# Experts in pairs with one branch between them, and one arm for the further tokens of both

## The chip, the cores and the metric

The kernel runs on one core of a Trainium2 chip. TensorE (PE) multiplies, VectorE (DVE) and ScalarE (ACT) work on what it leaves in the accumulators, GpSimd (POOL) does little here, and SyncE (SP) issues the DMA transfers. The metric is device time of one launch in microseconds (us), lower is better.

## The reference

Two layers over 256 tokens of width 1024. Each layer is an attention (differential in the first, stick-breaking in the second) and a layer norm, then a mixture of 32 experts and a layer norm. The change touches the experts alone:

```python
    g_prob = jax.nn.softmax((xt @ w_group + b_group).astype(f32), axis=-1)
    g_gate, g_idx = lax.top_k(g_prob, 1)
    ...
    e_gate, e_idx = lax.top_k(e_prob, MOE_TOP_K)
    ...
    def step(acc, ew):
        w1e, w3e, w2e, ge = ew
        h = jax.nn.silu(xt @ w1e) * (xt @ w3e)
        return acc + ge[:, None] * (h @ w2e).astype(f32), None
    y, _ = lax.scan(step, jnp.zeros((t, d), f32), (w1, w3, w2, gates.T))
```

Only the tokens with a gate above zero need an expert's work. How many these are is known on the chip alone, after the router. With the inputs of these runs the counts, which the reference's own router gives, are, for experts 0 to 31:

```
layer 0: 25 10 6 1 4 4 3 21 | 98 11 114 36 13 19 4 23 | 10 4 1 12 1 2 5 3 | 15 6 7 0 19 17 14 4
layer 1: 8 1 3 9 2 1 12 4 | 11 37 16 16 3 30 18 43 | 27 29 19 14 43 28 73 9 | 10 5 4 2 10 3 15 7
```

So in layer 0 experts 8 and 10 have over 96 tokens and expert 11 has 36; in layer 1 expert 22 has 73, and 9, 15 and 20 have 37 to 43. All the others fit into 32.

## The kernel before

**The stream.** An expert's weights are six tiles of 1 MB (w1, w3, w1, w3, w2, w2). Sixteen ring slots and four other places (T12, `wl`, `wh`, `x`) hold 20 tiles, a little over three experts. SP issues all transfers, in one fixed order. `refill` (line 148) hands each place that comes free to the next tile in the queue, so tile n stands in the place that tile n − 20 had, and SP waits at its issue until PE has read that older tile for the last time. Eight DMA semaphores are used in turn, so at most eight transfers are in flight.

**An expert.** The tokens that an expert serves are picked by a matmul with a matrix of ones and zeros (`oh`): `gather` (from line 840) does it for the 64 first tokens of each of four experts at once, after every fourth expert, and its marks `oh` are made by VectorE at line 843. Then PE multiplies into w1 and w3 ("up", line 923), VectorE and ScalarE copy the result, PE turns it (936), ScalarE and VectorE make silu times linear, PE multiplies into w2 ("down", 950), and the result with its gates is spread back over the tokens (`combine`, 872), one expert later for the short forms.

**The two forms and their branch.** There is a form for 32 tokens (64 matmuls of 128x256 up) and one for 64 (32 of 128x512). From expert 1 on each expert has a branch of its own (line 1093, on PE, ACT and DVE): over 32 tokens the 64-token form is run, and inside it, between up and the rest, `overflow` (line 1050) has a branch for over 64 tokens (1051), within it one for over 128 (1053) and one for over 192 (1055). An overflow gathers its 64 tokens (`gather_over`, 967) and runs the 64-token form on them, using the weights in their slots. `foresee` tells PE's sequencer ahead of time which way a branch will go (a hint); the branches at 1053 and 1055 have no hint. Expert 0 runs the 32-token form with no branch; its further tokens are done at expert 1 (`rest_of_first`), by a branch in which SP and its transfers take part.

A branch with all its transfers on SP makes SP wait at its end until all transfers in flight have landed:

```python
            n = count(0, ET.SP)
            with tc.If(n > 32):
                more(0, 32, w1, w3, w2, 32)
```

## Time and profile before

| | |
|---|---|
| median of 3 runs | 1286.6 us (1285.23 to 1286.78) |
| the profiled execution | 1279.04 us, its span 1277.3 us |
| granted clock of TensorE, mean of the span | 0.911 |
| moved by DMA | 443.12 MB |
| experts of layer 0, of layer 1 | about 152 to 642, 790 to 1262 us of the span |

The rows further below come from the profiled execution, with times in us from the start of its span. The experts of both layers are a steady stream of weights at around 0.41 MB a microsecond while the DMA engines are busy. The attention stages lie before 152, and between 642 and 790.

### The profile page before, as it was taken

What the parts mean: (1) busy time and instruction counts of PE and PEld (TensorE: products, weight loads), DVE (VectorE), ACT (ScalarE), POOL (GpSimd) and SP (SyncE); (2) the same over time, 40 slices, a digit from 0 to 9 for tenths busy, and PEclk for the clock granted to TensorE, in tenths of its full rate; (3) what the DMA queues carried; (4) which work ended last, traced back from release to release, by engine and by line L of the source; (5) the groups of instructions that cost most, each with busy time, mean ns of one, the idle gap of its engine ahead of it and who ended that gap; (6) DMA issues with size and microseconds to landing.
All of it is one profiled execution on the core that took longest, in us unless ns stands there. A gap on an engine that the chain in (4) does not pass through costs nothing. (4 is left out here: it accounts for less than half of the span.)

```text
span 1277.3 us, 21392 instructions
## 1 busy us (share of the span) xinstructions
PE 1028.1 (80%) x8502; PEld 631.0 (49%) x8502; DVE 401.9 (31%) x972; ACT 261.1 (20%) x625; POOL 143.5 (11%) x127
## 2 busy tenths in 40 slices
PE   8997887679877776877999998877867768866875
PEld 7886644434343443534468975444443434433542
DVE  5777612111121111213177766212121111111213
ACT  2344312111111111111112443111111111111111
POOL 4343000000000000004033320000000000000501
PEclk8998989898899878879999999979997998889898
DMA  7994689999499999999997337899999999999991
GB/s 251 353 374 158 201 323 414 413 372 389 168 365 411 415 406 411 410 409 416 404 383 282 127 123 279 303 412 413 402 416 398 408 408 410 415 396 399 386 411 44
DMA packets 102379, 443.12 MB, mean 347 GB/s; under 512 B 19016, under 2 KB 20080, under 8 KB 60288
## 3 DMA queue, kind: packets, MB, share of 16 engines
q1 hardware_dynamic: 102144, 439.98, 87.7%
q8 instruction: 148, 2.42, 0.8%
q14 instruction: 87, 0.71, 0.2%
HBM read 438.88 MB, written 1.06 MB: 344 GB/s over the span
## 5 line engine op out<-in xcount | busy, mean ns | idle before, releaser
L923 PE MATMUL bA<-w,T 128*32 128x256 f32 (+1 forms) x3128 | 285.4, 442 | 93.5 <-issue 51.9
L923 PEld LDWEIGHTS bA<-w,T 128*32 128x32 f32 (+1 forms) x3128 | 138.4, 123 | 212.1 <-issue 165.8
L950 PE MATMUL bY<-w,T 128*32 128x512 f32 (+1 forms) x864 | 138.7, 634 | 3.3 <-DVE T L944 1.9
L931 DVE COPY T<-bA 128x128 f32<-128x128 f32 (+1 forms) x64 | 19.6, 306 | 338.4 <-PE bA L923 292.8
L954 DVE SCALAR_TENSOR_TENSOR T<-bY,gv,T 128x512 fp32r<-128x512 f32 x64 | 48.1, 751 | 239.7 <-ACT T L953 239.7
L293 POOL TENSOR_TENSOR wl<-w,wh 128x512 fp32r<-128x512 f32 x66 | 86.8, 1316 | 187.8 <-DVE wh L292 82.5
L932 ACT COPY T<-bA 128x128 f32<-128x128 f32 (+1 forms) x64 | 17.7, 277 | 427.0 <-DVE T L931 422.2
L1006 POOL PARTITION_BROADCAST wh<-wh x8 | 5.6, 799 | 834.0 <-DMA wh<-in_ln_mix_b_dram 834.0
L856 PE MATMUL bA<-oh,xh 128*128 128x256 f32 x224 | 65.7, 323 | 31.5 <-DVE oh L843 30.5
L953 ACT ACTIVATE T<-bY,gv 128x512 fp32r<-128x512 f32 x64 | 44.0, 687 | 215.0 <-PE bY L950 215.0
L872 PE MATMUL bS<-T,gT 64*128 64x512 f32 x512 | 84.9, 449 | 0.7 <-DVE T L954 0.5
L856 PEld LDWEIGHTS bA<-oh,xh 128*128 128x128 f32 x224 | 48.9, 218 | 46.3 <-issue 42.5
L950 PEld LDWEIGHTS bY<-w,T 128*32 128x32 f32 (+1 forms) x864 | 31.2, 119 | 68.1 <-issue 48.4
L856 PE MATMUL bA<-oh,xl 128*128 128x256 f32 x224 | 63.5, 309 | 0.0
L293 DVE TENSOR_TENSOR wl<-w,wh 128x512 fp32r<-128x512 f32 x62 | 52.8, 851 | 19.2 <-ACT wh L292 17.3
L872 PEld LDWEIGHTS bS<-T,gT 64*128 64x128 f32 x512 | 47.3, 200 | 20.7 <-issue 12.5
L944 DVE TENSOR_TENSOR T<-T,bA 128x128 f32<-128x128 f32 (+1 forms) x64 | 19.3, 302 | 94.5 <-ACT T L943 94.5
L856 PEld LDWEIGHTS bA<-oh,xl 128*128 128x128 f32 x224 | 49.1, 219 | 0.0
L885 PE MATMUL bA<-ident,gg 128*128 128x128 f32 x128 | 30.3, 320 | 23.2 <-DVE T L931 14.7
L347 PE MATMUL bA<-xh,wh 128*128 128x256 f32 x160 | 47.1, 294 | 1.1 <-ACT xh L292 0.7
L349 PE MATMUL bA<-xl,wh 128*128 128x256 f32 x160 | 46.2, 289 | 0.9 <-DVE xl L293 0.9
L923 PE MATMUL bA<-T,T 128*32 128x256 f32 (+1 forms) x240 | 35.6, 444 | 13.4 <-issue 8.3
(301 smaller groups left out, 1690.5 us busy)
## 6 DMA issues: line engine op xcount, KB each, us to landing
w<-in_moe_w_dram SPq DMA_DIRECT2D x311, 1024.0 KB, 16.2
T<-in_moe_w_dram SPq DMA_DIRECT2D x48, 512.0 KB, 7.8
wl<-in_moe_w_dram SPq DMA_DIRECT2D x64, 256.0 KB, 12.0
wh<-in_moe_w_dram SPq DMA_DIRECT2D x64, 256.0 KB, 8.0
x<-in_moe_w_dram SPq DMA_DIRECT2D x16, 1024.0 KB, 9.5
w<-in_da_wk_dram SPq DMA_DIRECT2D x4, 1024.0 KB, 15.8
w<-in_da_wv_dram SPq DMA_DIRECT2D x4, 1024.0 KB
w<-in_da_wo_dram SPq DMA_DIRECT2D x4, 1024.0 KB, 15.2
```

What stands on the lines that cost most here:

```text
L293: lo.tensor_tensor(dl, src, dh.bitcast(F32), op=OP.subtract)
L347: nc.tensor.matmul(o, wh[:, cs], xh[:, k, :], start=k == 0 and cb % 2 == 0, stop=False, skip_group_check=True)
L349: nc.tensor.matmul(o, wh[:, cs], xl[:, k, :], start=False, stop=False, skip_group_check=True)
L856: nc.tensor.matmul(ps[:, kk * 256:kk * 256 + 256], part[:, t, c], oh[:, t].rearrange("p e c -> p (e c)"), start=n == 0, stop=n == 3)
L872: nc.tensor.matmul(acc[t][h], gT[r, t * P:(t + 1) * P], y[r, :], start=False, stop=last and y is yl, skip_group_check=True, tile_position= ...
L885: nc.tensor.transpose(ps[:, t * P:(t + 1) * P], gg[:, t], ident)
L923: nc.tensor.matmul(ps[j * C:(j + 1) * C, 0:W], xs(k), w(k % 4, j2 * W, (j2 + 1) * W), start=k == 0, stop=k == KC - 1, skip_group_check=Tru ...
L931: nc.vector.tensor_copy(ud[:, :, 0], us[:, :, :, 0])
L944: nc.vector.tensor_tensor(hT, s, pv[:, :, 64:P], op=OP.mult)
L950: nc.tensor.matmul(ps[j * C:(j + 1) * C, :], hT[:, c, q * C:(q + 1) * C], w2[m // 2](m % 2, h * 512, (h + 1) * 512), start=c == 0, stop=c ...
L953: nc.scalar.activation(yh, ps, AF.Copy, scale=gs)
L954: nc.vector.scalar_tensor_tensor(yl, ps, gs, yh.bitcast(F32), op0=OP.mult, op1=OP.subtract)
```

## The change

Experts go in pairs (even, odd). The even expert always runs the 32-token form with no branch, the odd one's branch asks whether either of the two has over 32 tokens. Where not, the odd one's 32-token form follows. Where so, the arm first does the even expert's further tokens (`rest(e - 1, ...)`), then the odd one's, and then the odd one's 32-token form. `rest` has three ways: up to 64 further tokens wanted (33 to 64 in all) a second 32-token run on the tokens that are already gathered; up to 96 one gather and one 64-token run; more (to 160) the arm v, with two gathers and two 64-token runs in turns. What is over 160 (or over 32 in expert 0) is done at expert 15, by a branch `z` over all experts in which SP takes part. `expert` is cut into `up`, `take_up`, `turn_up`, `glu`, `down` and `store`, so that `in_turns` can interleave two runs. Slots of the even expert are refilled behind the odd one, with the odd one's. The marks of a gather are made before the odd expert, and the gather runs behind it as before.

```diff
-        def gather(g):
+        def group_marks(g):
             oh = ph.tile([P, NT, GRP, CAP], F32R, name="oh")
             for t in range(NT):
                 nc.vector.tensor_tensor(oh[:, t], io[:, None, 0:CAP].to_broadcast([P, GRP, CAP]),
                                         pos[:, t, g * GRP:(g + 1) * GRP, None].to_broadcast([P, GRP, CAP]),
                                         op=OP.is_equal)
+            return oh
+
+        def gather(oh):
...
+        def in_turns(e, C, ggm, U, xm, w1, w3, w2, out):
+            pt = bankA()
+            turn_up(U[:, 0:HID], pt, HID)
+            pb = bankY()
+            up(e, CAP, lambda k: xm[:, k, :], w1, w3, pb, "m")
+            hT = glu(pt, U[:, 0:HID], HID)
+            outm = outputs(e, "m")
+            take_up(U[:, HID:], pb, HID)
+            gates(e, ggm, outm[0], outm[1], bankY)
+            pt = bankY()
+            turn_up(U[:, HID:], pt, HID)
+            ya = bankY()
+            down(CAP, hT, w2, ya)
+            hT = glu(pt, U[:, HID:], HID)
+            store(out, ya)
+            yb = bankY()
+            down(CAP, hT, w2, yb)
+            store(outm, yb)
+            return outm
...
+        def rest(e, n, xg, c0, w1, w3, w2, out, ahead=None):
+            with tc.If(n < CAP + 1):
+                foresee("u", e, n, CAP)
+                expert(e, 32, 32, lambda k: xg[k // 4][:, k % 4, c0 + 32:c0 + 64], w1, w3, w2, "", out)
+                combine(*out)
+            with tc.If(n > CAP, label=f"u{layer}_{e}"):
+                with tc.If(n < 32 + CAP + 1):
+                    foresee("v", e, n, 32 + CAP)
+                    more(e, 32, w1, w3, w2)
+                with tc.If(n > 32 + CAP, label=f"v{layer}_{e}"):
+                    if ahead is not None:
+                        ahead()
+                    oh = over_marks(e, io[:, 32:32 + CAP], CAP, "m")
+                    gg = marks(e, 32, CAP, "")
+                    both = blk(3, 2)
+                    xa = gather_over(oh, CAP, both[:, 0])
+                    over_marks(e, io[:, 32 + CAP:32 + 2 * CAP], CAP, "m", oh)
+                    ggm = marks(e, 32 + CAP, CAP, "m")
+                    pa = bankA()
+                    up(e, CAP, lambda k: xa[:, k, :], w1, w3, pa, "")
+                    U = blk(8, 1)[:, 0]
+                    take_up(U[:, 0:HID], pa, HID)
+                    xm = gather_over(oh, CAP, both[:, 1])
+                    gates(e, gg, out[0], out[1], bankA)
+                    outm = in_turns(e, CAP, ggm, U, xm, w1, w3, w2, out)
+                    combine(*out)
+                    combine(*outm)
...
+        def more(e, b0, w1, w3, w2, C=CAP, U=None, oh=None):
+            xg = gather_over(over_marks(e, io[:, b0:b0 + C], C, "m", oh), C)
...
-        cnt = sp.tile([1, N_EXP + 1], I32, name="cnt")
+        LIMIT = 32 + 2 * CAP
+        cnt = sp.tile([1, N_EXP + N_EXP // 2], I32, name="cnt")
         nc.vector.tensor_copy(cnt[:, 0:N_EXP], counts)
-        nc.vector.tensor_tensor(cnt[:, N_EXP:], cnt[:, 0:1], cnt[:, 1:2], op=OP.max)
-        xg, step0 = gather(0)
+        pairs = cnt[:, 0:N_EXP].rearrange("o (j i) -> o j i", i=2)
+        nc.vector.tensor_tensor(cnt[:, N_EXP:], pairs[:, :, 0], pairs[:, :, 1], op=OP.max)
+        xg, step0 = gather(group_marks(0))
...
-        def rest_of_first():
...
-        def overflow(e, n, w1, w3, w2):
-            with tc.If(n > CAP, label=f"o{layer}_{e}"):
-                more(e, CAP, w1, w3, w2)
-                with tc.If(n > 2 * CAP):
-                    more(e, 2 * CAP, w1, w3, w2)
-                    with tc.If(n > 3 * CAP):
-                        more(e, 3 * CAP, w1, w3, w2)
...
+            with tc.If(most > LIMIT, label=f"z{layer}_0"):
+                for e in range(N_EXP):
+                    w1, w3, w2 = [(again(e, j), again(e, k)) for j, k in ((0, 2), (1, 3), (4, 5))]
+                    n = count(e, ET.SP)
+                    with ExitStack() as inner:
+                        for b0, C in ((32, CAP), (32 + CAP, CAP), (LIMIT, CAP), (LIMIT + CAP, 32)):
+                            if e == 0 or b0 >= LIMIT:
+                                inner.enter_context(tc.If(n > b0))
+                                more(e, b0, w1, w3, w2, C)
...
+        def foresee_next(e):
+            if e == 15:
+                tc.mark_branch_hint_location(f"z{layer}_0", most > LIMIT, engines=[ET.PE])
+            else:
+                foresee("s", e + 2)
...
-            if 0 < e < N_EXP - 1:
-                ns[e + 1] = count(e + 1)
+            if e == 14:
+                most = count(N_EXP, ET.SP, limit=S + LIMIT - 32)
+            if e % 2 == 0 and e + 3 < N_EXP:
+                ns[e + 3] = count(N_EXP + e // 2 + 1)
             res = outputs(e, "")
+            if e % GRP == GRP - 1 and e + 1 < N_EXP:
+                oh_next = group_marks((e + 1) // GRP)
 
             def fill():
                 if done is not None:
@@ -1088,23 +1175,24 @@
                 foresee("s", 1)
                 hum(4)
                 run(32, first=first)
+            elif e % 2 == 0:
+                run(32)
+                before = w1, w3, w2
             else:
-                n = ns[e]
-                with tc.If(n > 32, label=f"s{layer}_{e}") as cmp:
-                    if e == 1:
-                        rest_of_first()
-                        n = count(1)
-
-                    def between():
-                        overflow(e, n, w1, w3, w2)
-                        foresee("s", e + 1)
-
-                    foresee("o", e, n)
-                    run(CAP, between=between)
+                with tc.If(ns[e] > 32, label=f"s{layer}_{e}") as cmp:
+                    n = count(e)
+                    if e > 1:
+                        n0 = count(e - 1)
+                        with tc.If(n0 > 32):
+                            rest(e - 1, n0, xg, c0 - CAP, *before, res, lambda: foresee("r", e, n))
+                    with tc.If(n > 32, label=f"r{layer}_{e}"):
+                        rest(e, n, xg, c0, w1, w3, w2, res)
+                    foresee_next(e)
+                    run(32)
                 with cmp.Else():
-                    foresee("s", e + 1)
+                    foresee_next(e)
                     run(32)
-            free_now = [p for p in freed(layer, e) if p in ("ring", "T12", "wl", "wh", "x")]
+            free_now += [p for p in freed(layer, e) if p in ("ring", "T12", "wl", "wh", "x")]
             if e == 0 and layer + 1 < DEPTH:
                 load_layer(layer + 1)
             if e == 29:
@@ -1112,9 +1200,19 @@
             if e + 2 == LAST_SPLIT:
                 finish_x()
                 gt = norm_rows("ln_ffn_", "wl", ("wh", "wl"))
-            refill(free_now)
+            if e % 2 or e == 0:
+                refill(free_now)
+                free_now = []
+            if e == 7:
+                t, u = cnt[:, N_EXP:N_EXP + 1], cnt[:, N_EXP + 1:N_EXP + 2]
+                nc.vector.reduce_max(t, cnt[:, 1:N_EXP], axis=AX.X)
+                nc.vector.tensor_scalar(u, cnt[:, 0:1], float(LIMIT - 32), None, op0=OP.add)
+                nc.vector.tensor_tensor(t, t, u, op=OP.max)
+            if e == 15:
+                leftovers(most)
+                foresee("s", e + 2)
             if e % GRP == GRP - 1 and e + 1 < N_EXP:
-                xg, step = gather((e + 1) // GRP)
+                xg, step = gather(oh_next)
                 for i in range(4):
                     step(i)
             done = res
```

What it moves on the engines, as the two programs' instruction lists have it.

**VectorE at the gather behind expert 7.** Before, the marks `oh` (line 843) stand right behind expert 7's arms and right ahead of the scaling of the gathered tokens (864), so they follow expert 7's last write:

```order
L931 COPY T_3936<-bA 128x128
L944 TENSOR_TENSOR T_3936<-T_3936,bA 128x128
L954 SCALAR_TENSOR_TENSOR T_3516<-bY,gv,T_3516 128x512
L1093 UNCONDITIONAL_BRANCH
L843 TENSOR_TENSOR oh<-io,pos 128x256 x2
L864 TENSOR_SCALAR T_3987<-bA,gp_141 128x256 x2
```

After the change they (line 842) stand behind expert 6's last write and ahead of the pair's branch (1182):

```order
L927 COPY T_4671<-bA 128x128
L938 TENSOR_TENSOR T_4671<-T_4671,bA 128x128
L955 SCALAR_TENSOR_TENSOR T_4632<-bY,gv,T_4632 128x512
L842 TENSOR_TENSOR oh<-io,pos 128x256 x2
L1182 COMPARE_AND_BRANCH
L1111 TENSOR_LOAD cnt x2
```

So the marks have moved ahead by a whole expert.

**VectorE in a heavy expert's arm.** Before, expert 8's arm: the branch at 1093, the marks `gg` of its first 64 tokens, the branch for over 64 (1051), the marks and the scaling of the second gather (959, 974), a whole 64-token run, and then the branch for over 128 (1053):

```order
L1093 COMPARE_AND_BRANCH
L878 TENSOR_SCALAR gg<-io,pos 128x128 x2
L1051 COMPARE_AND_BRANCH
L959 TENSOR_SCALAR ohm<-io,pos 128x64 x2
L974 TENSOR_SCALAR T_4076<-bY,gp_141 128x64 x4
L878 TENSOR_SCALAR ggm<-io,pos 128x128 x2
L931 COPY T_4141<-bY 128x2x128
L944 TENSOR_TENSOR T_4141<-T_4141,bY 128x256
L954 SCALAR_TENSOR_TENSOR T_4118<-bY,gvm,T_4118 128x512
L1053 COMPARE_AND_BRANCH
```

After the change, in the pair of experts 8 and 9, the same expert's arm v (behind the branches at 1186, 1006, 1010 and 1011, which on PE jump over the other two ways): the marks of both gathers, the scalings (1056), and two copies, two products and two writes:

```order
L1014 COMPARE_AND_BRANCH
L1036 TENSOR_SCALAR ohm<-io,pos 128x64 x2
L880 TENSOR_SCALAR gg<-io,pos 128x128 x2
L1056 TENSOR_SCALAR T_6053<-bY,gp_141 128x64 x4
L1036 TENSOR_SCALAR ohm<-io,pos 128x64 x2
L880 TENSOR_SCALAR ggm<-io,pos 128x128 x2
L927 COPY T_6117<-bA 128x2x128
L1056 TENSOR_SCALAR T_6053<-bY,gp_141 128x64 x4
L938 TENSOR_TENSOR T_6117<-T_6117,bA 128x256
L927 COPY T_6117<-bY 128x2x128
L938 TENSOR_TENSOR T_6117<-T_6117,bY 128x256
L955 SCALAR_TENSOR_TENSOR T_5831<-bY,gv,T_5831 128x512
```

The two 64-token runs stand in one arm now and take turns, where before one stood inside the other.

**SP at the branch for leftovers.** Before, it lies within expert 1, between the tile for `x` and those for `wh`; the second row is the way round it, with its wait for all eight semaphores of the transfers:

```order
L1093 UNCONDITIONAL_BRANCH
L1093 UNCONDITIONAL_BRANCH [waits SP_sequencer_49,DMAHW0_49,DMAHW1_49,DMAHW2_49,DMAHW3_49,DMAHW4_49,DMAHW5_49,DMAHW6_49,DMAHW7_49]
L102 DMA wh<-in_moe_w_dram 128x512 [waits DMAHW4_49]
L102 DMA wh<-in_moe_w_dram 128x512 [waits DMAHW5_49,PE_49]
L102 DMA wh<-in_moe_w_dram 128x512 [waits DMAHW6_49,PE_49]
```

After the change there is none at expert 1, and the same wait stands behind expert 15, ahead of the refills that follow it:

```order
L1124 UNCONDITIONAL_BRANCH [waits SP_sequencer_49,DMAHW0_49,DMAHW1_49,DMAHW2_49,DMAHW3_49,DMAHW4_49,DMAHW5_49,DMAHW6_49,DMAHW7_49]
L1182 UNCONDITIONAL_BRANCH
L80 DMA w<-in_moe_w_dram 128x2048 [waits DMAHW5_49,PE_49]
L80 DMA w<-in_moe_w_dram 128x2048 [waits DMAHW6_49,PE_49]
L80 DMA w<-in_moe_w_dram 128x2048 [waits DMAHW7_49]
```

So SP's wait for all transfers has moved from expert 1 to expert 15, in both layers.

## Rows read from the trace of the kernel before

**Rows 1.** The page: span, and the DMA engines' busy tenths in 40 slices.

```profile
span 1277.3 us, 21392 instructions
...
DMA  7994689999499999999997337899999999999991
```

**Rows 2.** Stretches: busy us (instructions) of PE, PEld, DVE, ACT, POOL; PEclk, DMA share, GB/s.

```profile
255.50:298.90 43.40, 33.58 (x164) 15.40 (x164) 5.60 (x17) 6.29 (x16) 0.00 (x0) 0.88 0.92 367
306.80:345.70 38.90, 32.71 (x170) 15.32 (x168) 5.67 (x16) 5.27 (x14) 0.00 (x0) 0.91 0.54 214
345.70:362.80 17.10, 14.55 (x68) 5.37 (x64) 2.02 (x5) 1.88 (x5) 0.00 (x0) 0.90 0.91 347
362.80:369.50 6.70, 4.39 (x32) 4.00 (x32) 3.51 (x8) 1.82 (x4) 0.00 (x0) 1.00 1.01 418
369.50:642.20 272.70, 212.68 (x2071) 117.79 (x2072) 48.21 (x123) 41.10 (x117) 21.07 (x20) 0.86 1.01 408
1100.30:1145.60 45.30, 34.96 (x168) 15.69 (x164) 6.43 (x17) 5.96 (x15) 0.00 (x0) 0.85 1.00 402
```

**Rows 3.** PE's timeline in expert 8 of layer 0: start, duration, line.

```profile
255.57 7.09 PE L923 MATMUL bA<-w,T 128*64 128x512 f32 x32
...
266.79 7.09 PE L923 MATMUL bY<-w,T 128*64 128x512 f32 x32 [0.44 <-DVE T L974]
...
276.45 3.65 PE L950 MATMUL bY<-w,T 128*64 128x512 f32 x16 [0.93 <-DVE T L944]
...
292.37 5.02 PE L950 MATMUL bY<-w,T 128*64 128x512 f32 x16
```

**Rows 4.** PE's timeline, starts of experts 9, 10 and 12.

```profile
298.94 3.66 PE L923 MATMUL bA<-w,T 128*32 128x256 f32 x64 [1.55 <-ACT T L953]
...
306.76 3.65 PE L923 MATMUL bA<-w,T 128*64 128x512 f32 x16
...
369.59 0.64 PE L923 MATMUL bA<-w,T 128*32 128x256 f32 x8 [0.25 <-DMA w<-in_moe_w_dram]
```

**Rows 5.** SP in layer 0: three issues of tiles; what two took to land.

```profile
L80 SPq DMA_DIRECT2D w<-in_moe_w_dram x1: 328/328/328, 235.2 to 235.2; - x1
DMA to landing us min/median/max: 21.1/21.1/21.1
...
371.54 1.68 SPq L80 DMA_DIRECT2D w<-in_moe_w_dram  x2
...
L80 SPq DMA_DIRECT2D w<-in_moe_w_dram x1: 328/328/328, 614.2 to 614.2; - x1
DMA to landing us min/median/max: 19.9/19.9/19.9
```

**Rows 6.** Each layer's last down on PE, and layer 1's last tiles on SP.

```profile
640.30 1.92 PE L950 MATMUL bY<-w,T 128*32 128x512 f32 x16
...
L80 SPq DMA_DIRECT2D w<-in_moe_w_dram x2: 327/471/615, 1231.0 to 1231.4; - x2
DMA to landing us min/median/max: 15.9/16.3/16.7
...
1260.01 1.92 PE L950 MATMUL bY<-w,T 128*32 128x512 f32 x16
```

**Rows 7.** PE's waits, 369 to 643 and (third row) 1100 to 1277: us, times, longest.

```profile
PE bA L923 <- issue: 31.3, 9, 5.5
PE bA L856 <- DVE oh L843: 9.3, 5, 2.2
...
PE bA L923 <- issue: 13.4, 5, 3.7
```

**Rows 8.** Branches on PE, both layers: ns least/median/most, first and last start.

```profile
L1053 PEldq COMPARE_BRANCH  x6: 187/1899/6066, 281.7 to 1134.2; - x6
...
L1093 PEldq COMPARE_BRANCH  x69: 82/1401/6167, 162.3 to 1248.3; - x69
```

**Rows 9.** SP's timeline at expert 1 of layer 0: the issues around the branch.

```profile
165.05 0.47 SPq L94 DMA_DIRECT2D x<-in_moe_w_dram  x1
174.48 0.33 SPq L102 DMA_DIRECT2D wh<-in_moe_w_dram  x1
```

More of the change, by code (lines that the diff above doesn't have):

```diff
@@ L108, in trunk @@
               "wh": load_split("wh")}
-    queue, late_items = [], [{} for _ in range(DEPTH)]
+    queue, items = [], [{} for _ in range(DEPTH)]
     LATE = {(0, 0): "T12", (0, 2): "T38", (0, 3): "T67", (0, 4): "wl", (0, 5): "x", (1, 0): "wh"}
@@ L157, in load_late @@
             if place in names:
-                loaded["moe", layer, *at] = places[place](*late_items[layer][at])
+                loaded["moe", layer, *at] = places[place](*items[layer][at])
                 used["moe", layer, *at] = place
@@ L221, in trunk @@
     nc.gpsimd.iota(order, pattern=[[-1, N_EXP]], base=N_EXP, channel_multiplier=0, allow_small_or_imprecise_dtypes=True)
-    mhalf = cp.tile([P, 16], F32, name="mhalf")
+    mhalf = cp.tile([P, 8], F32, name="mhalf")
     nc.vector.memset(mhalf, -0.5)
@@ L904, in hum, with up @@
                                  start=False, stop=False, skip_group_check=True)
-        def expert(e, b0, C, xs, w1, w3, w2, tag, out, fill=None, between=None, first=None):
-            gT, gs, yh, yl = out
-            bank = bankY if tag else bankA
+        def up(e, C, xs, w1, w3, ps, tag, first=None):
             nt = P // C
             W = 2 * HID // nt
-            gg = marks(e, b0, C, tag)
-            ps = bank()
             if first is not None:
@@ L924, in expert, with take_up @@
                                      start=k == 0, stop=k == KC - 1, skip_group_check=True, tile_position=(0, j * C))
-            if between is not None:
-                between()
-            U = blk(8, 1)[:, 0]
-            u = U[:, 0:HID]
+        def take_up(u, ps, W):
             ud = u[:, 0:W].rearrange("x (q c p) -> x q c p", c=2, p=P)
@@ L952, in expert, with store @@
                                      skip_group_check=True, tile_position=(0, j * C))
+        def store(out, ps):
+            gT, gs, yh, yl = out
             nc.scalar.activation(yh, ps, AF.Copy, scale=gs)
             nc.vector.scalar_tensor_tensor(yl, ps, gs, yh.bitcast(F32), op0=OP.mult, op1=OP.subtract)
-        def gather_over(e, ids, n, tag):
-            oh = ph.tile([P, NT, CAP], F32R, name="oh" + tag)[:, :, 0:n]
+        def expert(e, b0, C, xs, w1, w3, w2, tag, out, fill=None, between=None, first=None, U=None):
+            bank = bankY if tag else bankA
+            W = 2 * HID * C // P
+            gg = marks(e, b0, C, tag)
+            ps = bank()
+            up(e, C, xs, w1, w3, ps, tag, first)
+            if between is not None:
+                between()
+            if U is None:
+                U = blk(8, 1)[:, 0]
+            take_up(U[:, 0:HID], ps, W)
+            onward(e, C, gg, U, bank, w2, tag, out, fill)
@@ new lines, in onward @@
+        def onward(e, C, gg, U, bank, w2, tag, out, fill):
+            W = 2 * HID * C // P
+            gates(e, gg, out[0], out[1], bank)
+            ps = bank()
+            turn_up(U[:, 0:HID], ps, W)
+            if fill is not None:
+                fill()
+            if not tag:
+                stay(2, e)
+            hT = glu(ps, U[:, HID:], W)
+            ps = bankY()
+            down(C, hT, w2, ps)
+            store(out, ps)
+        def in_turns(e, C, ggm, U, xm, w1, w3, w2, out):
[17 more added lines that the diff above has]
+            return outm
@@ L1050, in overflow, with leftovers, again, w @@
-        def overflow(e, n, w1, w3, w2):
-            with tc.If(n > CAP, label=f"o{layer}_{e}"):
-                more(e, CAP, w1, w3, w2)
-                with tc.If(n > 2 * CAP):
-                    more(e, 2 * CAP, w1, w3, w2)
-                    with tc.If(n > 3 * CAP):
-                        more(e, 3 * CAP, w1, w3, w2)
+            return nc.values_load(cnt[0:1, e:e + 1], engines=engines, min_val=0, max_val=limit)
+        def leftovers(most):
+            def again(e, j):
+                src = items[layer][e, j][0]
+                def w(i, lo, hi):
+                    t = ph.tile([P, 512], F32, name="wm")[:, 0:hi - lo]
+                    nc.scalar.dma_start(t, src[:, i, lo:hi])
+                    return t
+                return w
+            with tc.If(most > LIMIT, label=f"z{layer}_0"):
[7 more added lines that the diff above has]
+                                more(e, b0, w1, w3, w2, C)
```

57 lines of the change are left out of this document (22 added, 35 removed).

## Prediction

> **What bounds the kernel now.** I read the page first: the span with the slices of the DMA share [rows 1]. The DMA engines are at 9 tenths or more in most slices of the two expert stages and low in the two attentions, and there is one more hole, a slice of 4 tenths at 319 to 351 us. The experts are thus bound by the stream of weights, except where TensorE (PE) holds the stream's slots too long. The table of stretches [rows 2] says where: through layer 0's expert 8 (255.5 to 298.9) the DMA share is still 0.92, in expert 10 (306.8 to 345.7) it falls to 0.54 at 214 GB/s, and from 369.5 on it is 1.01 to the end of the layer. So some 18 us of stream (0.46 x 38.9) are lost at experts 8 to 10, the two of layer 0 with over 96 tokens, because PE works there for 43.4 and 38.9 us on six tiles that arrive in 15 us (1.05 MB each at 0.41 MB/us). Expert 8 could not start much sooner: the tile behind its last two was issued at 235.2 and landed 21.1 later, at 256.3 [rows 5], so expert 8's last came at about 251.3, two tiles of 2.5 before.
>
> After that hole the order of arrival decides. SP issues tile 2 of expert 15 at 371.54, the moment the first slots of expert 12 come free [rows 5]; expert 12 itself starts at 369.59 [rows 4], behind the gather. From there everything to the end of layer 0 is that stream: the last tile issued at 614.2 lands 19.9 later, at 634.1 [rows 5], and PE ends at 640.30 + 1.92 = 642.2 [rows 6], 8.1 behind it. In layer 1 the stream has no such hole; its last tile, issued at 1231.4, lands at 1248.1, and PE ends the experts at 1261.9 [rows 6], 13.8 behind, because expert 22 (73 tokens) took 45.3 us [rows 2]. So three numbers set the result: when e12's slots come free in layer 0, how far PE ends behind the last tile, and how much of layer 1's last 13.8 us goes.
>
> **What the pieces cost.** A 32-token expert takes 7.8 us (298.94 to the next at 306.76) [rows 4]. In the 64-token form "up" takes 7.09; from its end (262.66) to the next "up" at 266.79 an overflow gather takes 4.13; from that one's end (273.88) to its "down" at 276.45 are 2.57; one "down" is 3.65 [rows 3].
>
> The new arm for 97 to 160 tokens (v) has two gathers, two ups, one turn (the other lies beside matmuls; I add 0.7), two downs and two combines of about 1.6 (280.10 to the next branch at 281.7 [rows 3, 8]): 8.3 + 14.2 + 2.6 + 0.7 + 7.3 + 3.2 = 36.3 us. To that comes the way in. PE has two branches there (n < 65 false, n < 97 false) that jump over a whole arm, and neither is announced to the sequencer. The nearest rows are the old branch inside an overflow, L1053: 0.19, 1.90 and 6.07 us (least, median, most), and the expert branch L1093: 0.08, 1.40 and 6.17 over 69 [rows 8]. After such a stop PE also runs slow: the down at 292.37 took 5.02 against 3.65 [rows 3], +1.4. I take 6 us an entry (one branch near the most, the other short), bounds 0.4 (two least ones) and 13 (two of the most and the slow stretch), and 0.7 for the way out. One v arm: 43 us.
>
> [...]
>
> **Layer 0 up to expert 12.** Expert 8 in the 32-token form waits for its own tiles: 251.3 + 1.9 (its down) = 253.2. Then v 43 to 296.2, expert 9 to 304.1, expert 10's 32-token run to 312.0, v 43 to 355.0. Expert 11 (36 tokens) now runs the 32-token form twice, one after the other: the rest 7.9 + 1.6 combine + 1.1 (turns with no matmuls beside them) = 10.6, + 1.5 for an announced branch, to 367.1; its own run to 375.0. The group's marks now stand before the odd expert, so the gather needs 4.6 in place of 6.7 (the 2.1 that PE waits for `oh` [rows 2, 7]): expert 12 starts at 379.6 against 369.59, +10. The price is that each heavy expert first does a 32-token run more (7.9, twice), its gain one combined arm instead of two passes with idle PE between them.
>
> **When e12's slots are free.** Before: at the end of the second part of its own up, 371.54. After the change the even expert's slots are released only by the first PE instruction of the odd expert's run, since the padding of the short arm is booked there, and they are refilled behind the odd expert in SP's queue. Expert 13 starts at 379.6 + 7.9 + about 1 for its branch = 388.5. So tile 2 of expert 15 is issued **17 us** later (with cheap branches 5, with dear ones 31). Behind it in the queue stands the whole stream of layer 0, which shifts to 634.1 + 17 = 651.1. PE's own path does not set the end: from 369.5 it has 272.7 us [rows 2], of which 9.3 wait for `oh` (now gone) and 31.3 for branches in 9 places [rows 7], about half of which go. That gives 379.6 + 272.7 − 9.3 − 15 = 628, below 651, so PE is then short of tiles and ends 2 to 4 us behind the last (down 1.92 and its turn): 654, against 642.2, **+12**. One more for slots of even experts that come too late once or twice: **+13**. All of attention 1 shifts with it, its weights being there.
>
> **Layer 1.** The stream has no hole there, so nothing up to expert 21 counts except what delays tiles (the pairs with 33 to 43 tokens cost PE about 3 us each against the 64-token form, hidden where PE waits for the stream). Expert 22: a 32-token run 7.9, a gather, one 64-token pass and a combine, 4.1 + 7.1 + 2.6 + 3.7 + 1.6 = 19.1, branches and way out 4 to 9: 31 to 36 in place of 45.3, −9. Two gathers in the tail −2.2 each [rows 7], and some of 13.4 us in 5 branch waits. Together over −13, but PE can't end sooner than 2 to 3 behind the last tile at 1248.1, so **−10** of 13.8 is what I take; bounds −4 (dear branches, tiles late) and −11.
>
> **The drain.** Before, the branch for expert 0's leftovers runs on SP at expert 1: all transfers land before SP goes on, 165.05 to 174.48 between two issues [rows 9]. It moves to expert 15 in both layers. Up to eight tiles were in flight, so most of these 9.4 us are stream time; what is lost is the start of an empty queue, which I estimate at 2 us in either place, and the early one is gone: 0; with what more there is of code and of late even slots in layer 1 **+2**, bounds 0 and +6. The smaller `mhalf` and the maximum of the counts cost nothing that I can see: three operations on one row of VectorE, once a layer, behind an expert that is waiting for tiles.
>
> **Sum.** 13 − 10 + 2 = +5 on the profiled execution's 1279.04: 1284.0. The median of the runs shown lies 7.6 above the profiled one; 1286.6 + 5 = 1291.6, say **1292 us**. The same sum runs from about −8 to +26 with the bounds of the branches alone.
>
> **Rivals.**
> *A, branches are cheap (faster).* If each unannounced branch costs what the least of its kind did, 0.19 [rows 8], an entry costs 0.4: two of them save 11.2, the rest of 11 another 1. Expert 12 starts before 369, its slots are free 5 us later than before, the stream ends at 639 and PE at 642: 0 in layer 0. With −10 or −11 and +2: 1278. For it: the least rows; VectorE and ScalarE pass the same branches in well under 0.1 us. Against it: the median of 1.40 and 1.90 on PE. It decides from an entry below about 3 us. [...]
> *B, branches are dear (slower).* With 13 an entry and 6 for expert 11, expert 12 starts 18 later still, layer 0 ends at +31, layer 1 gains less: 1286.6 + 31 − 7 + 2 = 1312.
> *C, the stream starves in every pair.* Even slots come free one expert (8 to 15 us) later, and 20 places hold little more than three experts. If each of the ten pairs behind expert 12 loses 2 us, layer 0 alone gives +20 more, 1311. Eight transfers in flight cover 20 us, which speaks against it; it decides when an odd expert starts over 20 us after the even one's tiles were used up.
> *D, nothing measurable.* An entry of 3.5 us gives layer 0 +8, layer 1 −10 and the rest +2: 1286.6. Loss and gain are of one size, so this is a matter of 2 or 3 us an entry.
>
> **How the numbers follow.** Slightly slower, 1289.2 to 1304, as in the sum: 0.40. B or C, above 1304: 0.20. A: 0.24. D: 0.16, where "within 0.2%" is 2.6 us, about what the measurement of this kernel can tell. So faster 0.24, same 0.16, slower 0.60. The range begins at A's own time, which leaves about half of A out (0.12), and ends at those of C and B (0.07 beyond): 1278 to 1311. The forecast's own range is 1289 to 1304.
>
> **What would show it.** In the trace after: PE starts expert 8 before 250 and its v arm at about 253 to 260; the two unannounced branches on PE take together about 5 us; expert 12's first matmul stands at 376 to 383; SP's issue for expert 15's third tile stands at about 388; the DMA hole at 320 to 335 is longer, not shorter; the last tile of layer 0 lands near 651 and PE ends within 4 us of it; PE waits for `w` oftener, for `oh` never; layer 1's experts end 2 to 4 us behind their last tile. Wrong would be: expert 12 before 372 (then A), the even experts' slots free with their own last matmul (then the stream loses 8 less), or a stream in layer 1 with gaps (then C).

## The result, and the profile after

The changed kernel takes 1306.4 us in the median of 4 runs (1305.1 to 1306.6), the kernel before 1286.7 (1285.2 to 1289.4): ratio 1.0165, 95% interval 1.0131 to 1.0198. That is slower, the way that was forecast, and inside the range of 1278 to 1311; but it is +20 where the sum said +5, and above 1304, the upper end of the forecast's own range, where the prediction had put a chance of 0.20 (B or C). The profiled execution took 1306.58, that of before 1279.04, which is 7.6 under its kernel's median; so the rows of the two differ by 27.5 us, not by 20.

The page of the changed kernel, first its span and the DMA engines' busy tenths:

```profile
span 1304.8 us, 22936 instructions
...
DMA  8984699959068989999999536799999989988993
```

Against [rows 1] the hole in layer 0 is two slices long and reaches down to 0 (slices 11 and 12, 326 to 391 us), and slice 9 (261 to 294), in expert 8's arm, has only 5 tenths. The stretches of PE's work from expert 8 to expert 12 (columns as in [rows 2]) say who is at it:

```profile
247.90:298.10 50.20, 42.67 (x196) 23.26 (x196) 8.22 (x23) 7.37 (x19) 0.00 (x0) 0.76 0.66 265
298.10:314.20 16.10, 9.68 (x102) 5.10 (x104) 1.06 (x4) 0.98 (x4) 0.00 (x0) 0.79 1.01 421
314.20:327.00 12.80, 9.63 (x100) 5.04 (x92) 1.82 (x5) 1.66 (x5) 0.00 (x0) 0.87 1.00 419
327.00:370.80 43.80, 38.55 (x197) 21.09 (x198) 9.28 (x27) 7.37 (x19) 0.00 (x0) 0.84 0.33 120
370.80:393.50 22.70, 17.36 (x195) 9.04 (x193) 2.39 (x7) 2.64 (x9) 0.00 (x0) 0.92 0.48 159
393.50:398.40 4.90, 4.27 (x34) 3.86 (x32) 2.69 (x6) 1.80 (x4) 0.00 (x0) 1.00 1.00 415
```

The lines are expert 8's arm, expert 9, expert 10's 32-token run, its arm, expert 11 and the gather. The granted clock is 0.76 in the first, as a mean over the stop at its start and the work behind it. PE's timeline shows the stops (start, duration, line; in brackets the idle time ahead and who ended it):

```profile
254.43 0.61 PE L1049 MATMUL bY<-ohm,xh 128*128 128x64 f32 x2 [6.56 <-DVE ohm L1036]
...
261.94 9.91 PE L921 MATMUL bA<-w,T 128*64 128x512 f32 x32 [0.50 <-DVE T L1056]
...
288.44 7.09 PE L948 MATMUL bY<-w,T 128*64 128x512 f32 x32
...
304.46 5.69 PE L921 MATMUL bA<-w,T 128*32 128x256 f32 x64 [6.34 <-DVE gg L880]
...
331.22 0.61 PE L1049 MATMUL bY<-ohm,xh 128*128 128x64 f32 x2 [4.25 <-DVE ohm L1036]
...
398.41 3.66 PE L921 MATMUL bA<-w,T 128*32 128x256 f32 x64
```

PE stops for 6.56 us at the way into expert 8's arm, for 6.34 at the way out and for 4.25 at the way into expert 10's, and after each stop the same work takes longer: up in the 64-token form 9.91 in place of 7.09 [rows 3], in the 32-token form 5.69 in place of 3.66 [rows 4]. The granted clock in pieces of expert 8's arm (third number from the end) says when:

```profile
254.40:262.00 7.60, 7.07 (x34) 6.97 (x36) 0.61 (x3) 0.09 (x1) 0.00 (x0) 0.50 1.01 424
268.00:270.00 2.00, 2.00 (x12) 0.60 (x10) 0.00 (x0) 0.00 (x0) 0.00 (x0) 1.00 1.04 420
276.00:278.00 2.00, 2.00 (x11) 2.00 (x12) 0.69 (x2) 0.79 (x2) 0.00 (x0) 0.50 0.94 382
```

It is 0.50 from the first gather to 267 or 268, in the first half of the first up, then 1.00, and 0.50 once more from 274.5 to 281, in the second gather and the second up. PE did not stop ahead of this second stretch, so the stops do not account for all of the half clock.

VectorE's marks, named as releaser, are not the cause: they themselves wait for PE's branch, as the view of that line shows (ns least/median/most; the second row is the branch out of expert 8's arm alone; the last line is who waited for the line longest, with us and times):

```profile
L1188 PEldq COMPARE_BRANCH  x6: 73/3112/6875, 297.6 to 1178.9; - x6
...
L1188 PEldq COMPARE_BRANCH  x1: 6216/6216/6216, 297.6 to 297.6; - x1
...
  DVE gg L880: 28.5, 3
```

The same for the jump over the ways for up to 96 tokens and for the branch over the leftovers:

```profile
L1011 PEldq COMPARE_BRANCH  x4: 68/1674/5351, 248.4 to 1177.5; - x4
...
L1124 PEldq COMPARE_BRANCH  x2: 5557/5579/5601, 428.3 to 1041.4; - x2
```

VectorE passed the branch at 1188 in 43 to 69 ns. SP issues expert 15's third tile at 406.71 (371.54 in [rows 5]), and both layers end as follows (the issue of a late tile each, the second with its landing time, and the last down):

```profile
406.71 1.28 SPq L80 DMA_DIRECT2D w<-in_moe_w_dram  x3
...
L80 SPq DMA_DIRECT2D w<-in_moe_w_dram x1: 328/328/328, 650.6 to 650.6; - x1
...
670.97 2.11 PE L948 MATMUL bY<-w,T 128*32 128x512 f32 x16
...
L80 SPq DMA_DIRECT2D w<-in_moe_w_dram x1: 328/328/328, 1261.5 to 1261.5; - x1
...
DMA to landing us min/median/max: 20.5/20.5/20.5
...
1287.72 1.92 PE L948 MATMUL bY<-w,T 128*32 128x512 f32 x16
```

Third tile of expert 15 +35.2 us, last tile of layer 0 issued at 650.6, +36.4, last down's end 673.1, +30.9: the chain of slots, stream and end that the prediction followed, at two to two and a half times its size (+17, +17 and +12). In layer 1 the tile issued at 1261.5 landed at 1282.0; two more follow it, the last at about 1284 (an estimate from the spacing of the issues); PE ends at 1289.6, about 5 behind (13.8 before).

### The profile page after: what moved, and what is told of

Same layout as the page of the kernel before. It is cut to its first block, busy times and chain, and to the rows that moved or that the text cites. A ratio compares the mean times of both kernels' runs of the same rounds, so it can differ in the third digit from the quotient of the medians.

```text
span 1304.8 us, 22936 instructions
## 1 busy us (share of the span) xinstructions
PE 1065.2 (82%) x9292; PEld 653.9 (50%) x9292; DVE 411.6 (32%) x1020; ACT 273.2 (21%) x663; POOL 143.6 (11%) x127
## 5 line engine op out<-in xcount | busy, mean ns | idle before, releaser
L921 PE MATMUL bA<-w,T 128*32 128x256 f32 (+1 forms) x3608 | 301.2, 424 | 110.5 <-DMA w<-in_moe_w_dram 41.5
L921 PEld LDWEIGHTS bA<-w,T 128*32 128x32 f32 (+1 forms) x3608 | 145.9, 120 | 241.7 <-issue 124.9
L955 DVE SCALAR_TENSOR_TENSOR T<-bY,gv,T 128x512 fp32r<-128x512 f32 x70 | 52.6, 751 | 239.2 <-ACT T L954 227.9
L928 ACT COPY T<-bA 128x128 f32<-128x128 f32 (+1 forms) x70 | 18.8, 268 | 461.1 <-DVE T L927 456.1
L954 ACT ACTIVATE T<-bY,gv 128x512 fp32r<-128x512 f32 x70 | 48.1, 687 | 211.4 <-PE bY L948 207.9
L858 PE MATMUL bA<-oh,xh 128*128 128x256 f32 x224 | 60.5, 305 | 19.2 <-PEq L1124 12.0
L858 PEld LDWEIGHTS bA<-oh,xh 128*128 128x128 f32 x224 | 44.7, 200 | 33.2 <-issue 24.1
L880 DVE TENSOR_SCALAR gg<-io,pos 128x128 f32<-128x128 f32 x140 | 36.6, 305 | 67.3 <-PEq L1188 28.5
L858 PE MATMUL bA<-oh,xl 128*128 128x256 f32 x224 | 57.5, 292 | 0.0
L349 PE MATMUL bA<-xh,wl 128*128 128x256 f32 x160 | 46.8, 292 | 0.0
L921 PE MATMUL bA<-wh,T 128*32 128x256 f32 x208 | 30.2, 432 | 20.3 <-DVE gg L880 13.4
## 6 DMA issues: line engine op xcount, KB each, us to landing
w<-in_da_wk_dram SPq DMA_DIRECT2D x4, 1024.0 KB, 13.8
```

Of the source, the lines that this page charges most:

```text
L349: nc.tensor.matmul(o, wl[:, cs], xh[:, k, :], start=False, stop=k == KC - 1, skip_group_check=True)
L858: nc.tensor.matmul(ps[:, kk * 256:kk * 256 + 256], part[:, t, c], oh[:, t].rearrange("p e c -> p (e c)"), start=n == 0, stop=n == 3)
L880: nc.vector.tensor_scalar(gg[:, t], io[:, None, b0:b0 + C].to_broadcast([P, P // C, C]), pos[:, t, e:e + 1], None, op0=OP.is_equal)
L921: nc.tensor.matmul(ps[j * C:(j + 1) * C, 0:W], xs(k), w(k % 4, j2 * W, (j2 + 1) * W), start=k == 0, stop=k == KC - 1, skip_group_check=Tru ...
L954: nc.scalar.activation(yh, ps, AF.Copy, scale=gs)
L955: nc.vector.scalar_tensor_tensor(yl, ps, gs, yh.bitcast(F32), op0=OP.mult, op1=OP.subtract)
```

## Experiments

Theory S (stops): what the change loses, it loses by PE's long jumps into and out of the arms and the half clock behind them. Rivals: P, the slots of even experts that come free late; W, the arms' further work (a 32-token run ahead of each heavy arm, serial second runs); and the moved drain. All kernels ran beside the kernel before, whose median was 1286.7, 1285.1 and 1286.3 us in the three groups.

| kernel | median us | ratio to before, 95% |
|---|---|---|
| p_no_arms: changed, no arm entered | 1226.2 | 0.9524 (0.9477 to 0.9570) |
| s_no_arms: before, no arm entered | 1238.3 | 0.9622 (0.9575 to 0.9669) |
| p_late_hint | 1309.4 | 1.0170 (1.0130 to 1.0210) |
| p_no_z | 1291.2 | 1.0043 (1.0014 to 1.0072) |
| p_taken_ways | 1259.3 | 0.9803 (0.9777 to 0.9828) |
| p_ahead | 1272.1 | 0.9915 (0.9882 to 0.9948) |
| s_marks_last | 1274.4 | 0.9915 (0.9886 to 0.9944) |
| s_early_marks | 1270.6 | 0.9892 (0.9866 to 0.9918) |
| s_shift: before, 64 short matmuls more at its start | 1292.5 | 1.0051 (1.0016 to 1.0087) |
| p_shift: changed, 64 short matmuls more at its start | 1288.3 | 1.0037 (1.0011 to 1.0062) |
| p_taken_no_z | 1250.6 | 0.9732 (0.9699 to 0.9765) |
| p_ahead_hint | 1275.7 | 0.9907 (0.9873 to 0.9942) |

**No arms at all (p_no_arms, s_no_arms).** The same line in both kernels:

```diff
-        nc.vector.tensor_copy(cnt[:, 0:N_EXP], counts)
+        nc.vector.tensor_scalar(cnt[:, 0:N_EXP], counts, 32.0, None, op0=OP.min)
```

> The changed kernel with the token counts cut to 32 before the branches, so that no further tokens are done (tokens over 32 of an expert are left out) and no arm is entered; what is left is the pairs: the even expert's slots released at the odd one, the marks ahead of the gather, the drain at expert 15. Theory S (stops): the loss is made in the arms, by PE's long jumps into and out of them and the half clock behind each; then the pairs alone cost no more than 4 us against the kernel before cut in the same way: about 1243 us, the stream without a hole in both layers. Rival P (pairs): slots of even experts that come free late starve the stream; then 1 to 2 us in each of 30 pairs, 1265 or more, with gaps in the DMA in every pair.

> The kernel before with the same cut at 32 tokens (tokens over 32 are left out). Layer 0's hole at experts 8 to 12 (28 us of stream) is gone and PE ends each layer 2 to 3 us behind its last tile: 1286.7 - 28 - 5 - 11 = about 1243 us. Under S the two cut kernels differ by less than 4 us; under P the pairs are 20 us or more behind this one.

The kernel with pairs is 12 us faster than the one with single branches, not 4 us slower at most: P falls. The DMA rows of the two, pairs first, have no hole behind expert 8 in either:

```profile
DMA  8994689999999799999996447999999979999993
...
L1182 PEldq COMPARE_BRANCH  x32: 342/372/5746, 162.2 to 1191.9; - x32
```

```profile
DMA  8994679999999999999996347899999999999993
...
L1093 PEldq COMPARE_BRANCH  x62: 337/1212/5977, 161.3 to 1202.7; - x62
```

Half as many branches on PE, with a median of 0.37 against 1.21 us. That the 12 us are the pairs' is not shown: the marks ahead of the gather and the moved branch for leftovers are in this kernel too, and its code lies elsewhere. What differs as well is the stream where it sets the pace (pairs first; the last number is GB/s, the one before it the DMA share):

```profile
500.00:600.00 100.00, 78.66 (x660) 38.27 (x660) 17.21 (x39) 12.43 (x35) 21.17 (x20) 0.83 1.01 420
...
500.00:600.00 100.00, 74.66 (x664) 35.66 (x664) 15.63 (x39) 12.72 (x35) 20.91 (x20) 0.93 1.01 412
```

The DMA engines are busy throughout in both, but move 2% more in the one with pairs. Over two stages of some 450 us that is an estimated 17 us, more than the 12. Why the stream is faster stays open.

The cut changes one operation on VectorE in each kernel. So the arms cost the changed kernel 1306.4 − 1226.2 = 80 us and the kernel before 1286.7 − 1238.3 = 48: the loss is in them.

**The ways that are taken, without branches inside (p_taken_ways).** In the six pairs whose arm is entered:

```diff
-                    n = count(e)
-                    ...
-                    with tc.If(n > 32, label=f"r{layer}_{e}"):
-                        rest(e, n, xg, c0, w1, w3, w2, res)
+                    if (layer, e) in TAKEN:
+                        way0, way = TAKEN[layer, e]
+                        if way0:
+                            only(way0, e - 1, xg, c0 - CAP, *before, res)
+                        if way:
+                            only(way, e, xg, c0, w1, w3, w2, res)
```

> The changed kernel; the branch of each pair stays, but in the six pairs whose arm is entered with these inputs the arm holds only the ways that are taken (expert 8: 97 to 160; 10: the same, and 11: 33 to 64; in layer 1 experts 9, 15 and 20: 33 to 64, 22: 65 to 96), with no branches inside; the other ways are left out there. PE's work is the same. S (stops): the nine jumps of 1.3 to 6.9 us inside the arms are gone with most of the half clock behind them; expert 12 of layer 0 starts at 368 to 376 in place of 398, and the kernel takes 1265 to 1280 us. Rival W (work): the further 32-token runs ahead of the heavy arms and the serial second runs are what costs it; then expert 12 starts at 390 or later and the kernel takes 1295 us or more.

The same work of PE, 47 us less, and less than the 1265 to 1280 that S gave. Its timeline and SP's issue of expert 15's third tile:

```profile
289.20 3.66 PE L921 MATMUL bA<-w,T 128*32 128x256 f32 x64
...
369.62 3.66 PE L921 MATMUL bA<-w,T 128*32 128x256 f32 x64
...
377.91 1.28 SPq L80 DMA_DIRECT2D w<-in_moe_w_dram  x3
```

Expert 9 starts 15.3 us earlier than in the changed kernel, expert 12 28.8, and the tile's issue comes 28.8 earlier. W falls: with the 32-token runs and the serial second runs still there, expert 12 starts where it did before the change (369.59, [rows 4]). The edit takes out the inner branches and the code of the ways not taken at once, so which of the two costs is not told apart.

But the half clock did not all go with the stops. Here only 1.80 us lie ahead of expert 8's first further gather, and the clock falls in that gather all the same (the gather's start, the first up, and a stretch with the granted clock):

```profile
250.18 0.46 PE L1078 MATMUL bY<-ohm,xh 128*128 128x64 f32 x2 [1.80 <-DVE ohm L1065]
...
256.80 9.45 PE L921 MATMUL bA<-w,T 128*64 128x512 f32 x32 [0.53 <-DVE T L1085]
...
255.00:260.00 5.00, 4.47 (x14) 2.27 (x16) 2.09 (x8) 1.62 (x4) 0.00 (x0) 0.50 1.02 433
```

The first up takes 9.45 us, nearly as in the changed kernel; the second is back at 7.09. From expert 8's last down to expert 9's up 40.8 us pass in place of 56.6: the way in is 4.8 shorter, the body 4.7 and the way out 6.3.

**The place of the hint (p_late_hint).**

```diff
-                    if ahead is not None:
-                        ahead()
...
+            if ahead is not None:
+                ahead()
             yb = bankY()
             down(CAP, hT, w2, yb)
```

> The changed kernel with one line moved: in the arm for 97 to 160 tokens the hint for the branch behind it (whether the odd expert has further tokens) stands ahead of the arm's last down instead of at the arm's head, some 8 us ahead of the branch and not 43. S, in the form that the early hint's fetch is overwritten by the arm's own code: the branch out of expert 8's arm falls from 6.2 us to under 1.5, expert 9 runs at full clock, expert 12 starts 7 to 10 us earlier and the kernel takes 1296 to 1300 us. If the stop has nothing to do with when the hint is given: 1306 us and the branch again takes 6 us.

A miss: no faster, and the branch out of expert 8's arm took 6.08 us, though the hint had been executed 9 us ahead of it (at 287.0):

```profile
L1309 PEldq BRANCH_PREFETCH_HINT  x2: 35/38/40, 287.0 to 302.4; - x2
...
L1188 PEldq COMPARE_BRANCH  x1: 6080/6080/6080, 296.0 to 296.0; - x1
```

That the hint came too early is thus not the reason; that the arm's code overwrites what the hint fetches was the author's supposition, and no row shows it. Why the hint does nothing here stays open.

**The leftovers' branch (p_no_z), alone and with the ways (p_taken_no_z).** The edit takes out `leftovers(most)`, its count and its maximum.

```diff
             if e == 15:
-                leftovers(most)
                 foresee("s", e + 2)
```

> The changed kernel without the branch for what is over 160 tokens (work that these inputs do not have). S: it only takes the drain at expert 15 and the jump over that code away, 2 to 3 us a layer, PE being 2 us behind the stream at the end of layer 0: 1300 to 1304 us. If the moved drain were the main cost: 1290 us or less.

> Both at once: only the ways that are taken in the six arms (the other ways left out) and no branch for over 160 tokens (work that these inputs do not have). If the two losses add up: 1259 less 12 to 15, 1244 to 1248 us; 1255 or more if the leftovers' branch only cost what the arms had made late.

15 us less in one, where 2 to 6 were expected, and 9 in the other, where 12 to 15 were. PE's two jumps over that code took 5.56 and 5.60 us (the row at 1124 above). What SP's drain takes from the stream can be read by itself, in the stretch around it in each layer, first in the changed kernel and then without the branch (the last two numbers are DMA share and GB/s):

```profile
425.00:485.00 60.00, 43.53 (x427) 22.95 (x418) 9.64 (x26) 8.69 (x24) 0.00 (x0) 0.87 0.90 366
1010.00:1090.00 80.00, 56.48 (x596) 32.33 (x600) 13.92 (x38) 11.39 (x34) 0.00 (x0) 0.85 0.92 377
...
425.00:485.00 60.00, 47.08 (x446) 24.08 (x445) 9.72 (x27) 9.40 (x25) 0.00 (x0) 0.91 1.02 419
1010.00:1090.00 80.00, 65.40 (x711) 36.81 (x712) 15.66 (x43) 14.40 (x40) 0.00 (x0) 0.94 1.01 415
```

That is about 7 us of stream in each layer. It is there in every trace with the branch (a share of 0.91 to 0.94 in p_late_hint, p_taken_ways and p_shift) and in neither without it (1.01 in p_taken_no_z), so it is no matter of placement. In layer 0 a part comes back: from 500 to 600 us the stream moves 421 GB/s in the changed kernel and 409 in p_no_z, and why stays open. But see the next pair: what stands behind this code in memory moves with it, so neither difference in time is the branch's price alone. The 1291 us are close to the 1290 that the moved drain as the main cost would have given; but p_taken_ways, with the drain still in it, takes 1259.

**The same code at other addresses (s_shift, p_shift).** A control, for both kernels: 64 short matmuls (8 columns, on zeros) more at the start, so that all later code of PE lies further on.

```diff
     warm(WARM_START)
+    pad = bankA()
+    for _ in range(64):
+        nc.tensor.matmul(pad[:, 0:8], zerob, zerob[:, 0:8], start=True, stop=False, skip_group_check=True)
```

> [...]

> The same control on the changed kernel: 64 short matmuls more at the start. If the stops into and out of the arms depend on where the code lies by chance, some of the 5.4, 6.2 and 3.1 us around expert 8's and 10's arms shrink or grow by us and the time moves by up to 10 us; if they are a matter of the jump's distance alone, the same stops within 1 us and 1303 to 1309 us.

The largest surprise: the changed kernel with nothing but its code moved takes 18 us less, 1288.3, more than the 10 at most that were expected; the kernel before takes 6 more. The long branches on PE, those of over 1.2 us added up over the trace, go the same way: from 89 us in 23 to 76 in 18 in the changed kernel, from 146 us in 43 to 173 in 44 in the kernel before. The branch out of expert 8's arm, and then expert 9, the first matmul of expert 12 and the tile of expert 15, in the moved kernel:

```profile
L1191 PEldq COMPARE_BRANCH  x1: 350/350/350, 291.5 to 291.5; - x1
...
292.76 1.06 PE L924 MATMUL bA<-w,T 128*32 128x256 f32 x15 [0.60 <-DVE gg L883]
297.92 4.95 PE L924 MATMUL bA<-w,T 128*32 128x256 f32 x49 [4.10 <-issue]
...
384.81 3.66 PE L924 MATMUL bA<-w,T 128*32 128x256 f32 x64
...
394.31 1.65 SPq L80 DMA_DIRECT2D w<-in_moe_w_dram  x3
```

6.22 us have become 0.35, of which 4.10 come back in the middle of expert 9's up; expert 12 starts 13.6 earlier. The way out is the smaller part of this: it and expert 9 together are 1.4 us shorter, the body of expert 8's arm 3.8 (its second up takes 7.09), expert 10's 32-token run 5.0 (the stop of 3.1 us in it is gone), and PE was 2.0 ahead before the arm. Other stops stayed (the branch into expert 8's arm: 5.23). So a stop's size is not that of its jump alone, it hangs on where the code lies, and of the 20 us measured for the change up to 18 are the luck of one placement. By two placements each, the change is worth +20 or +2 against the kernel before, +14 or −4 against that one moved.

**Other arrangements (s_early_marks, s_marks_last, p_ahead, p_ahead_hint).** The marks of the gather alone, in the kernel before:

```diff
             res = outputs(e, "")
+            if e % GRP == GRP - 1 and e + 1 < N_EXP:
+                oh_next = group_marks((e + 1) // GRP)
...
-                xg, step = gather((e + 1) // GRP)
+                xg, step = gather(oh_next)
```

> The kernel before with the marks ahead of the gather alone. Expert 12's slots come free 2 us sooner and layer 1's tail has two gathers at 2.2 us less each: 1280 us; same as before within 2 us if all of it is hidden.

1270.6, faster than both kernels. Its profiled execution took 1271.8, 7 us less than that of before, as expected; the rest of the 14 is not explained by the two traces. PE's waits for `oh` at line 856, 30.5 us in 15 before, are gone, but expert 12 starts no sooner (370.85 for 369.59). This kernel was run in one placement only, and its long branches on PE add up to 128 us in 32, against 146 in 43; so how much of the gain is the marks' and how much is luck is not shown.

> The kernel before, a branch for each expert, with two parts of the change that need no pairs: marks ahead of the gather, and the branch for expert 0's further tokens moved from expert 1 to expert 31 (in the arm of expert 31). 5 us from the early drain in layer 0, 2 from expert 12's earlier start, 4 in the tail: about 1275 us; 1283 or more if the stream's lead at expert 8 is worth nothing.

The time is the one expected (1274.4, from 1266.8 to 1282.0), but not by the terms given: next to the marks alone nothing more is won with the leftovers moved to expert 31, though the early drain is gone.

The branch ahead of the pair, in the loop of the kernel before:

```diff
+                with tc.If(ns[a0] > 32, label=f"s{layer}_{a0}") as cmp:
+                    ...
+                        for e in es:
+                            with tc.If(nn[e] > 32) as inner:
+                                wide(e, nn[e])
+                            with inner.Else():
+                                one(e, 32)
+                        foresee("s", z0 + 1)
+                with cmp.Else():
+                    foresee("s", z0 + 1)
+                    for e in es:
+                        one(e, 32)
```

> Pairs with the branch ahead of both: the kernel before with one branch for each pair (2 and 3, 4 and 5, up to 30 and 31), where neither has over 32 tokens the two 32-token runs stand one behind the other; where one has, the arm holds for each of the two the old branch and the old 64-token form with its overflow. The marks of a gather are made ahead, expert 0's further tokens are done in the arm of the last pair, and an odd expert's result is spread right behind its pair. S: pairs keep what they gained without arms (12 us with the drain and the leftovers' jump in it) and the heavy experts cost what they cost before: 1262 to 1275 us, faster than both. W's view of pairs says the same of the heavy experts; if the pairs' gain came from the 32-token runs of even experts that need no branch in any case, 1283 or more.

As expected, 1272.1: a pair need not run a heavy expert twice to save its branch. But the marks alone gave 1270.6, so a gain of the pairs is not shown by it. The next one gives the hint ahead of the second expert (`wide(e, nn[e], ahead)`, and ahead of `one` in the else arm):

> The kernel with the branch ahead of the pair, with the hint for the next pair's branch given before the second expert's down rather than at the end of the arm. S with hints that work: the jumps behind the heavy pairs (6.0, 5.4 and 5.9 us in layer 0, six more in layer 1) fall below 2 and the kernel takes 1260 to 1267 us; as in the changed kernel, where the hint's place did not matter: 1272 us.

No gain, the second time that a hint's place made no difference: the long jumps behind the heavy experts of layer 0 took 5.7, 5.7 and 6.0 us where they had taken 6.0, 5.4 and 5.9.

## Why the prediction was right, and where it was wrong

**Right: what bounds it.** The end of layer 0 hangs on when expert 12's slots come free. This was +35.2, the last tile +36.4, PE about 2 behind it (2 to 4 forecast; the tile's landing is estimated by the 20.9 us of the two ahead of it). Attention 1 shifted along. But expert 12's first matmul, at 398.4, lies outside the 376 to 383 that was to show the forecast.

**Mis-sized: the arms.** Forecast were 43 us an arm with 6 for the way in and 0.7 for the way out. Measured were 56.6 from the end of expert 8's 32-token run (247.9) to expert 9's up (304.5): the way in 6.6 (right), the body 43.7 where 36.3 were summed from rows at full clock (+7.4), the way out 6.3 (+5.6). Then expert 9 took 9.7 for 7.9, expert 10's 32-token run with a stop of 3.1 in its up 12.8 for 7.9, the second arm 43.8 for 43, expert 11 22.7 for 20, the gather 4.9 for 4.6. Against that expert 8 was done 5.3 earlier than forecast. Sum: 13.6 + 1.8 + 4.9 + 0.8 + 2.7 + 0.3 − 5.3 = 18.8, from 379.6 to 398.4. The slots were a further 8.3 behind it, as forecast. Three terms failed. The way out was priced as an announced branch, an estimate that no row gave, and the hint bought nothing (6.22 us). The half clock was counted once an entry (1.4), where the granted clock was 0.50 for 13 us behind the way in and for 7 more with no stop ahead of them. And the stop inside expert 10's run, with the half clock behind it (4.9 together), was put at nothing. p_taken_ways shows the way in, the way out and the second stretch of half clock together, by more than a placement was seen to change; the first stretch stays in it, and what makes it is open. p_shift shows that the way out and the stop in expert 10 hang on the placement: that both fell into this one is bad luck, not something the sum could have had.

**Mis-sized: the leftovers' branch.** 2 us were put for moved drain and code together, 6 at most. The 2 us for the start of an empty queue came from no row; the traces show about 7 us of stream at expert 15 in each layer, and PE's jump over the code of 32 experts takes 5.6 us in each. Without the branch the kernels took 15 and 9 us less, with placement in both numbers.

**Mis-sized: the tail.** PE came 8 to 9 us nearer to its last tile of layer 1 (10 forecast). But expert 22's pair held PE for 42.8 us (1142.9 to 1185.7) where 31 to 36 were forecast, 7.2 of them the way out, and the stream, which was to have no hole there, lost about 5: its last tile came 36 us later than before, after a start that was about 31 later. So layer 1 gave back 3 us (PE's end moved by 30.9 in layer 0 and by 27.7 in layer 1), not 10, and less than the bound of 4.

**The rivals.** C, starving pairs, was wrong: without arms the kernel with pairs is the faster one. A's condition, cheap branches, was not met, but its direction is what p_taken_ways shows: 1259, even below the 1278 given. B, dear branches, had the kind of loss, and 1306 lies nearer to its 1312 than to the forecast; but its entry of 13 us was not met (6.6 and 4.3 measured), and the loss came from the terms above. That p_shift's 1288.3 is close to the 1291.6 forecast is luck: expert 12 starts at 384.8 there, 5 us behind the forecast, and the terms differ from those of the sum.

What PE waits for in a long jump no run shows. p_shift shows that the price hangs on where the code lies: 64 matmuls more on PE, with their weight loads, turned 6.22 us into 0.35. And a branch on PE has no one price: the median at the pairs' branch was 0.37 us even where no arm was entered (from 0.34 to 5.75 in 32, p_no_arms). VectorE and ScalarE took 0.03 to 0.07, as the prediction had it (at line 1093 of the kernel before 41 to 72 and 33 to 55 ns, 69 times each).

## What to carry to other kernels

Price a branch on PE from traces, on the way out of an arm as well as in, and as a range: the same branch took 6.22 and 0.35 us here with its code in two places. Add the half clock (0.50 for 13 us and for 7 more in one arm here), but look at the granted clock piece by piece before it is put down to a stop. A hint is no reason to price a branch at nothing until a trace shows so: with one, in two places, the way out took 6.22 and 6.08 us here. A branch that makes SP wait for all transfers is paid for in stream, here about 7 us each time it lay where the stream set the pace. Where a kernel has many such branches, run it with its code moved, more than once, before a difference of a per cent is put down to the change. And look for the small part of a large change that may pay by itself: here the gather's marks moved ahead, which were faster than both kernels in the one placement that was run.

## What the runs had that was not expected

Moving PE's code by 64 short matmuls at the start, with no other difference, changed the time by −18 us in one kernel and +6 in the other. Single jumps on PE went from 6.22 to 0.35 us by it, while VectorE and ScalarE passed the same branches in 33 to 72 ns in every row read. In the 50 us that begin with the stop of 6.6 us the granted clock was 0.76 in the mean, 0.50 in two stretches of which the second followed on no stop, and in p_taken_ways it fell to 0.50 in the same gather behind a wait of only 1.8 us.
